# First stage of a two-layer decoder: raw input transposed, the norm's factors moved to the weights' split and to the evictions, half of the reordering on ScalarE

## The chip, the cores and the metric

One core of one Trainium2 chip runs the whole kernel in one launch. The metric is the device time of an execution in microseconds; the time before is the median of three runs. Durations are those of one profiled execution.

## What is computed

Two decoder layers over x (512 tokens, 1024 features, fp32). The change concerns the beginning of layer 0: the norm of x, and the projection to q, k and v with `w_qkv` for 12 heads in three groups of four.

```
def rms_norm(x, g):
    y = x32 * rsqrt(mean(x32 * x32, axis=-1) + EPS)
    return y * g
...
qkv = rms_norm(h, g[0]) @ w_qkv          # 1024 -> 3 * 768
q, k = rope(q), rope(k)                   # first 16 of 64 features of a head
# three groups of heads, (window, dilation) = (128,1), (512,4), (2048,16):
# banded softmax attention within each residue class of the dilation
o = concat(o_g * softmax over groups of the log denominators) @ w_o
h = h + rms_norm(o, g[1])
h = h + rms_norm(conv_ffn(rms_norm(h, g[2])), g[3])
# then a shared K/V and forget gates, forgetting attention, a second conv_ffn
```

## The kernel before

Every engine works through its own queue in order, and the order of the program's lines is the order of each queue (`manual_schedule`); waits between engines are semaphores that the framework puts in. SyncE issues nearly all loads.

**Precision.** A product of fp32 operands is made of three products in a rounded format (`mm3`, L263 to L266): each operand is split in a high part (a rounding copy on ScalarE) and a low part (operand less high part, on VectorE); the three are high·high, high·low and low·high.

**Weights.** `Weights` (L35 to L100) holds a list of pieces of 128x1024 fp32 (512 KB). `load` issues the transfers of a piece, `high` makes the high part on ScalarE (L57), `low` the low part on VectorE (L69), `split(n)` does both up to piece n, and `get` hands out the next pair after splitting `ahead` - 1 further ones. Pieces 0 to 3 are group 0's q and k columns (two chunks of 128 rows, kc, and 512 columns each), 4 and 5 group 0's v (four chunks of 256 columns each), 6 to 9 group 1's q and k, 10 to 13 group 2's, 14 to 17 the v of both.

**The start (L1252 to L1289).** x comes in four blocks of 128 tokens (`load_x`), in turn with the first pieces. The gain row is spread over 128 partitions by four products with a row of ones (L252); products of zeros before and after them (`warm_up`) keep TensorE busy. Per block b, `rstd_h` takes square, root and reciprocal, `normed` (L298) multiplies h by factor and gain on VectorE, `transpose_in` (L348) transposes the result on TensorE in two halves and splits each into xT's high part (ScalarE, L355) and low part (VectorE, L356). `qk0(b, pieces)` adds up block b's q and k of group 0 over the eight chunks. `qk_post` (L1071) copies them out on ScalarE and rotates on GpSimd.

**Groups 1 and 2** take the tokens by residue: `reorder` writes xT as xP, in which the tokens with the same remainder modulo 4 stand together. It is 16 copies of 128x512 that read every fourth element, all on GpSimd (L1060): blocks 0 and 1 after the second `qk_post`, blocks 2 and 3 after the last.

**What follows.** `v_proj0` makes group 0's v, and between its blocks the transposes of q and k (`qk_transpose`, copied out by VectorE at L1089). Then come the scores of blocks 0 and 1 (L1111; their softmax on VectorE L1096 and ScalarE L1097), group 1's q and k (`wide_proj(1)`), group 2's, and both v's. `down_sums` prepares sums of later weights all the while: SyncE loads, VectorE takes differences (L580 to L583), SyncE writes back. PSUM has eight banks for everything.

Of the kernel before, what the change touches and what calls it, by code (L numbers as in the profile page):

```python
# [9 lines left out]
F32 = mybir.dt.float32  # L10
# [5 lines left out]
D = 1024  # L16
T = 512
# [17 lines left out]
class Weights:  # L35
# [3 lines left out]
    def __init__(self, nc, new_raw, new_pair, pieces):  # L39
        self.nc, self.new_raw, self.new_pair, self.pieces = nc, new_raw, new_pair, pieces  # L40
        self.ahead, self.ahead_dma = 4, 2
        self.raw, self.ready, self.half_done = {}, {}, []
        self.n_dma = self.n_split = self.n_get = 0

# [8 lines left out]
    def high(self, minus=False):  # L53
        if self.n_split < len(self.pieces):
            self.load(self.n_split + 1 + self.ahead_dma)
            raw, pair = self.raw.pop(self.n_split), self.new_pair()
            self.nc.scalar.copy(pair[:, 0], raw)  # L57
            self.half_done.append((raw, pair))
            if minus:
                self.minus()  # L60
# [5 lines left out]
    def low(self):  # L66
        if self.half_done:
            raw, pair = self.half_done.pop()
            self.nc.vector.tensor_tensor(pair[:, 1], raw, pair[:, 0].bitcast(F32), ALU.subtract)  # L69
            self.ready[self.n_split] = (pair[:, 0], pair[:, 1])  # L70
            self.n_split += 1

# [31 lines left out]
def trunk_kernel(ctx, tc, x, norm_gains, w_qkv_a, w_o_a, w_q_b, w_o_b, kv_norm, w_kvf, b_f,  # L104
# [38 lines left out]
    for g in range(3):  # L143
        for s in range(4):
            def f(raw, g=g, s=s):
                v = raw.rearrange("p (k c) -> p k c", k=2)
                return [(v[:, :, 0:256], cols(wqkv, 2 * s, 2, g * 256, 256)),
                        (v[:, :, 256:512], cols(wqkv, 2 * s, 2, 768 + g * 256, 256))]
# [68 lines left out]

    eps_t = cst.tile([128, 1], F32, name="eps_t")
    dve.memset(eps_t, EPS)
    g_row = t4([1, D], name="g_row")  # L220
    sp.dma_start(g_row, norm_gains[0:1, 0, :])
    ones = sml.tile([1, 128], F32R, tag="ones", name="ones", bufs=1)
    dve.memset(ones.bitcast(F32), 1.0)

    zero = t2([128, 512], BF16, name="zero")
    dve.memset(zero, 0.0)
# [2 lines left out]
    def warm_up(n):  # L229
        for i in range(n):  # L230
            pe.matmul(warm, zero[:, 0:128], zero, start=True, stop=True)
# [10 lines left out]
    ident = cst.tile([128, 128], F32, name="ident")  # L242
    make_identity(nc, ident)

    gr = t4([1, D], F32R, name="gain_h"), t4([1, D], F32R, name="gain_l")
    dve.tensor_copy(gr[0], g_row)
    dve.tensor_tensor(gr[1], g_row, gr[0].bitcast(F32), ALU.subtract)
# [20 lines left out]
    def rstd_h(b, between=None):  # L268
        ss = small(1, "s1")
        junk = t2([128, D], BF16, name="junk")  # L270
        act.activation(junk, h[:, b, :], AF.Square, scale=1.0 / 32, accum_out=ss)
        sd = small(1, "sd")
        act.activation(sd, ss, AF.Sqrt, bias=eps_t)
        if between is not None:
            between()
        r = small(1, "rs")
        dve.reciprocal(r, sd)
        return r

    def rstd_shared(b):  # L280

        ss, s2 = small(1, "s1"), small(1, "vr")
        junk, junk2 = (t2([128, 512], BF16, name="junk") for _ in range(2))
        act.activation(junk, h[:, b, 0:512], AF.Square, scale=1.0 / 32, accum_out=ss)
        dve.scalar_tensor_tensor(junk2, h[:, b, 512:1024], 1.0 / 1024, h[:, b, 512:1024], ALU.mult, ALU.mult,
                                 accum_out=s2)
        dve.tensor_scalar(s2, s2, EPS, None, ALU.add)
        sd, r = small(1, "sd"), small(1, "rs")
        act.activation(sd, ss, AF.Sqrt, bias=s2)
        dve.reciprocal(r, sd)  # L290
        return r

# [752 lines left out]

    xT = new_xT("xa")
    xP = new_xT("xp")
    xn = {}

    def by_fourth(a, spec="p k (l r) -> p k r l"):  # L1050
        return a.rearrange(spec, r=4)

    def reorder(*blocks):
# [13 lines left out]
    def qk_post(g, b, o):  # L1067
        if b == 0:
            qks[g] = t8([128, 4, 8, HD], name=f"qk{g}")
        qk = qks[g][:, b]  # L1070
        act.copy(qk.rearrange("p a d -> p (a d)"), o)  # L1071
# [137 lines left out]
    def v_proj0(between):  # L1209
        banks = []  # L1210
        ws = [[t.rearrange("p (k c) -> p k c", k=4) for t in W.get()] for _ in range(2)]
        for b in range(4):
            if b % 2 == 0:
                banks.append(bank([128, 2, 256], name="v_ps"))
            for kc in range(KD):
                wh, wl = ws[kc // 4]
                ah, al = ax(0, b, kc)
                mm3(banks[b // 2][:, b % 2, :], ah, al, wh[:, kc % 4, :], wl[:, kc % 4, :],
                    kc == 0, kc == KD - 1)
            if b == 1:  # L1220
                V[0] = t4([128, 4, 256], name="V0")
            if b % 2:
                act.copy(V[0][:, b - 1:b + 1, :], banks[b // 2])
                for f in between[b // 2]:
                    f()

# [4 lines left out]
    W.ahead = 1  # L1231
    ws, qk_banks = {}, {}

    def norm0(b):
        xn[b] = normed(b, rstd_h(b), gain0)

    def transpose0(b, between=None):
        transpose_in(b, xn.pop(b), xT, between)

    def qk0(b, *pieces):  # L1240
        if b not in qk_banks:
            qk_banks[b] = bank([128, T], name="qk_ps")
        for s in pieces:
# [3 lines left out]
            for k in range(2):  # L1247
                kc = 2 * s + k
                ah, al = ax(0, b, kc)
                mm3(qk_banks[b], ah, al, wh[:, k, :], wl[:, k, :], kc == 0, kc == KD - 1)  # L1250

    xn[0] = normed(0, rstd_shared(0), gain0)  # L1252
    W.split(1)
    transpose0(0, L(W.split, 2))
    qk0(0, 0)
    W.high()
    r1 = rstd_h(1, W.low)
    qk0(0, 1)
    W.high()
    xn[1] = normed(1, r1, gain0)  # L1260
    W.low()
    qk0(0, 2)
    transpose0(1)
    qk0(0, 3)
    norm0(2)
    qk_post(0, 0, qk_banks[0])
    qk0(1, 0, 1, 2)
    transpose0(2)
    dve.tensor_reduce(same, ident.rearrange("p (a c) -> p c a", c=4), axis=mybir.AxisListType.X, op=ALU.add)
    dve.tensor_scalar(same, same, -NEG, NEG, ALU.mult, ALU.add)  # L1270
    dve.tensor_tensor(mask2.rearrange("p (a c) -> p a c", c=4),
                      mask0[:, 128:256].rearrange("p (a c) -> p a c", c=4),
                      same[:, None, :].to_broadcast([128, 32, 4]), ALU.add)
    norm0(3)
    qk0(1, 3)
    qk_post(0, 1, qk_banks[1])
    reorder(0, 1)
    qk0(2, 0, 1)
    transpose0(3)
    qk0(2, 2, 3)  # L1280
    W.split(5)
    qk_post(0, 2, qk_banks[2])
    qk0(3, 0, 1, 2, 3)
    W.ahead = 4
    W.split(6)
    qk_post(0, 3, qk_banks[3])
    sums = down_sums([(1, 6), (1, 7)], in_two, sp, 1, 3)
    next(sums)
    reorder(2, 3)  # L1289

    def wide_proj(g, name, post, between):

        banks = [bank([128, T], name=name) for _ in range(4)]
# [14 lines left out]
    def v_post(g, b, o):  # L1308
        if b == 0:
            for i in (1, 2):  # L1310
                V[i] = t4([128, 4, 256], name=f"V{i}")
        act.copy(V[1][:, b, :], o[:, 0:256])
        dve.tensor_copy(V[2][:, b, :], o[:, 256:512])
# [437 lines left out]
```

## Time and profile before

| | |
|---|---|
| time, median of 3 runs | 1112.1 us (1111.95 to 1112.55) |
| profiled execution | 1112.53 us |
| its span | 1110.8 us |
| TensorE busy | 1101.9 us (99%) |
| VectorE busy | 876.8 us (79%) |
| ScalarE busy | 660.6 us (59%) |
| GpSimd busy | 214.9 us (19%) |
| first product with a weight | 9.17 us |
| first product of group 0's v | 35.16 us |

A row of a timeline gives the start in us, the time in us, engine, line, operation, what is written from what, the shape and the count; in brackets stands how long the engine sat idle before it and what ended that. A row of the groups gives the busy time in us, the mean of one in ns, and the idle time before them. PE is TensorE, PEld its weight loads, DVE VectorE, ACT ScalarE, POOL GpSimd, SP SyncE.

### The profile page before, as it was taken

How to read it: one execution, taken by the hardware profiler on the slowest of the kernel's cores; microseconds unless marked ns; L12 is line 12 of the kernel's file. 1: busy time of each engine (PE TensorE's matmuls, PEld its weight loads, DVE VectorE, ACT ScalarE, POOL GpSimd, SP SyncE). 2: the span in 40 equal slices, each digit the busy share in tenths (PEclk: the TensorE clock that was granted, in tenths of full speed). 3: DMA queues.
4: the chain of work that ended last, by engine and by line, in shares of the span. 5: the costliest groups of instructions: out<-in, count | busy, mean ns of one | idle time of the engine just before them, and what ended most of it. 6: DMA issues, size and time to landing. Idle time of an engine off the chain costs nothing.

```text
span 1110.8 us, 18056 instructions
## 1 busy us (share of the span) xinstructions
PE 1101.9 (99%) x6610; PEld 952.9 (86%) x6610; DVE 876.8 (79%) x1484; ACT 660.6 (59%) x1088; POOL 214.9 (19%) x313
## 2 busy tenths in 40 slices
PE   9999999999999999999999999999999999999997
PEld 6988889899999988888878788789999999988886
DVE  6587788888788689997686676868887787779894
ACT  5444565656666747576451587756556666747572
POOL 2832001311111211000000455500411111211000
PEclk9999999999999999999999999999999999999999
DMA  9599864468878979894448434593379888989872
GB/s 325 173 340 410 325 181 135 86 180 191 210 190 185 249 254 321 292 324 112 133 152 281 163 107 119 169 286 114 83 180 212 192 186 193 229 265 322 315 246 76
DMA packets 184242, 236.26 MB, mean 213 GB/s; under 512 B 11673, under 2 KB 131465, under 8 KB 184154
## 3 DMA queue, kind: packets, MB, share of 16 engines
q1 hardware_dynamic: 169210, 182.94, 50.6%
q0 software_dynamic: 14944, 52.18, 20.6%
q8 instruction: 52, 0.85, 0.3%
q14 instruction: 36, 0.29, 0.1%
HBM read 166.08 MB, written 39.63 MB: 185 GB/s over the span
## 4 chain that ended last, share of the span: by engine, by line
PE 94%; DVE 2%; DMA 1%; issue 1%; ACT 1%; POOL 1%; DVEq 0%; SPq 0%; POOLq 0%; ACTq 0%
PE up L266 12%; PE up L265 12%; PE up L264 12%; PE acc L264 8%; PE acc L265 8%; PE acc L266 8%; PE v_ps L264 2%; PE v_ps L266 2%; PE v_ps L265 2%; PE qk_ps L265 2%; PE qk_ps L264 2%; PE qk_ps L266 2%; PE q_ps L264 1%; PE first L266 1%; PE first L264 1%; PE first L265 1%
## 5 line engine op out<-in xcount | busy, mean ns | idle before, releaser
L264 PE MATMUL acc<-w 128*128 128x512 f32 (+1 forms) x311 | 120.6, 388 | 0.3 <-DVE mix L326 0.3
L266 PE MATMUL acc<-w 128*128 128x512 f32 (+1 forms) x311 | 120.4, 387 | 0.0
L69 DVE TENSOR_TENSOR w<-wraw,w 128x1024 fp32r<-128x1024 f32 x74 | 97.5, 1334 | 27.1 <-ACT w L57 26.7
L57 ACT CAST w<-wraw 128x1024 fp32r<-128x1024 f32 x94 | 96.9, 1050 | 22.7 <-PE v_ps L265 6.9
L265 PE MATMUL acc<-w 128*128 128x512 f32 (+1 forms) x267 | 103.2, 387 | 0.0
L266 PE MATMUL up<-xsh,w 128*128 128x256 f32 x352 | 99.7, 283 | 0.1
L264 PE MATMUL up<-xsh,w 128*128 128x256 f32 x352 | 99.6, 283 | 0.0
L265 PE MATMUL up<-xsl,w 128*128 128x256 f32 x352 | 99.6, 283 | 0.0
L614 ACT ACTIVATE bb<-up,conv 128x512 f32<-128x512 f32 x80 | 59.7, 776 | 59.0 <-DVE up L1001 48.2
L265 PE MATMUL up<-xbl,w 128*128 128x512 f32 (+1 forms) x276 | 93.5, 339 | 0.0
L265 PE MATMUL up<-xcl,w 128*128 128x512 f32 (+1 forms) x276 | 93.5, 339 | 0.0
L264 PE MATMUL up<-xbh,w 128*128 128x512 f32 (+1 forms) x276 | 93.5, 339 | 0.0
L266 PE MATMUL up<-xbh,w 128*128 128x512 f32 (+1 forms) x276 | 93.5, 339 | 0.0
L264 PE MATMUL up<-xch,w 128*128 128x512 f32 (+1 forms) x276 | 93.5, 339 | 0.0
L266 PE MATMUL up<-xch,w 128*128 128x512 f32 (+1 forms) x276 | 93.4, 338 | 0.0
L264 PEld LDWEIGHTS acc<-w 128*128 128x128 f32 x311 | 58.4, 188 | 12.6 <-DVE mix L326 0.7
L266 PEld LDWEIGHTS acc<-w 128*128 128x128 f32 x311 | 58.4, 188 | 11.9
L266 PEld LDWEIGHTS up<-xsh,w 128*128 128x128 f32 x352 | 67.6, 192 | 0.3 <-DMA w<-wsum 0.3
L265 PEld LDWEIGHTS up<-xsl,w 128*128 128x128 f32 x352 | 67.6, 192 | 0.0
L264 PEld LDWEIGHTS up<-xsh,w 128*128 128x128 f32 x352 | 67.6, 192 | 0.0
L615 DVE SCALAR_TENSOR_TENSOR bb<-up,conv,bb 128x511 f32<-128x511 f32 x80 | 59.5, 744 | 6.2 <-ACT bb L614 6.0
L617 DVE SCALAR_TENSOR_TENSOR bb<-up,conv,bb 128x510 f32<-128x510 f32 x80 | 59.9, 749 | 2.8
(313 smaller groups left out, 3118.7 us busy)
## 6 DMA issues: line engine op xcount, KB each, us to landing
wraw<-in_w_up_dram SPq DMA_DIRECT2D x88, 512.0 KB, 5.6
w<-wraw POOLq DMA_DIRECT2D x32, 512.0 KB, 6.4
dT<-dsums SPq DMA_DIRECT2D x28, 512.0 KB, 7.6
w<-wsum POOLq DMA_DIRECT2D x24, 512.0 KB, 5.8
dsums<-in_w_down_dram SPq DMA_DIRECT2D x22, 512.0 KB, 7.6
dsums<-in_w_down_dram SPq DMA_DIRECT2D x44, 256.0 KB, 5.5
hD<-hc POOLq DMA_DIRECT2D x44, 256.0 KB, 6.9
dact<-hD SPq DMA_DIRECT2D x44, 256.0 KB, 5.6
```

Source lines behind the costliest of these rows:

```text
L57: self.nc.scalar.copy(pair[:, 0], raw)
L69: self.nc.vector.tensor_tensor(pair[:, 1], raw, pair[:, 0].bitcast(F32), ALU.subtract)
L264: pe.matmul(o, ah, bh, start=first, stop=False, skip_group_check=shared)
L265: pe.matmul(o, ah, bl, start=False, stop=False, skip_group_check=shared)
L266: pe.matmul(o, al, bh, start=False, stop=last, skip_group_check=shared)
L614: act.activation(bb[:, s, :], ps, AF.Identity, bias=cp[:, 3, ch:ch + 1], scale=cp[:, 2, ch:ch + 1])
L615: dve.scalar_tensor_tensor(bb[:, s, 1:], ps[:, :T - 1], cp[:, 1, ch:ch + 1], bb[:, s, 1:], ALU.mult, ALU.add)
L617: dve.scalar_tensor_tensor(bb[:, s, 2:], ps[:, :T - 2], cp[:, 0, ch:ch + 1], bb[:, s, 2:], ALU.mult, ALU.add)
```

## The change

x is transposed as it lands. The gain, which belongs to a feature, goes into the split of the weights of group 0, 1 and 2 (pieces 0 to 17): a piece is split chunk by chunk, the high part by an activation with the chunk's gains as scale, the low part by a scalar-tensor-tensor. The gains come as eight columns through one small transpose. The reciprocal root, which belongs to a token, goes into the evictions of q, k and v as a scale; for groups 1 and 2 it takes a round trip through DRAM (`factors_out`) to come in the order of xP. The pieces of q and k are loaded as two transfers by chunk instead of by q and k. TensorE's order of the first products is by chunks over blocks 0 and 1; pieces 4 and 5 are split before the third block; blocks 2 and 3 are reordered by ScalarE.

```
@@ Weights.high / Weights.low
-            self.nc.scalar.copy(pair[:, 0], raw)
+            scales = self.scales.get(self.n_split)
+            if scales is None:
+                self.nc.scalar.copy(pair[:, 0], raw)
+            else:
+                for i, g in enumerate(scales):
+                    s = slice(i * 1024 // len(scales), (i + 1) * 1024 // len(scales))
+                    self.nc.scalar.activation(pair[:, 0, s], raw[:, s], AF.Identity, scale=g)
...
+                    self.nc.vector.scalar_tensor_tensor(pair[:, 1, s], raw[:, s], g, pair[:, 0, s].bitcast(F32),
+                                                        ALU.mult, ALU.subtract)
@@ loads and gains
     load_x(0)
+    W.load(2)
+    load_x(1)
     W.load(3)
-    load_x(1)
+    load_x(2)
     W.load(4)
-    load_x(2)
...
-    gain0 = [bank([128, 512], name="gain00") for _ in range(2)]
-    warm_up(4)
-    for part in range(2):
-        for i in range(2):
-            pe.matmul(gain0[i], ones, gr[part][:, i * 512:(i + 1) * 512], start=part == 0, stop=part == 1)
-    warm_up(4)
+    warm_up(3)
+    pg0 = bank([128, 8], name="g_ps")
+    pe.transpose(pg0, g_row, ident[:8, :8])
+    gcol0 = sml.tile([128, 8], F32, tag="gcol0", name="gcol0", bufs=1)
+    dve.tensor_copy(gcol0, pg0)
+    warm_up(5)
...
+    for s in range(4):
+        for n in (s, 6 + s, 10 + s, 14 + s):
+            W.scales[n] = columns(2 * s, 2 * s + 1)
+    for s in range(2):
+        W.scales[4 + s] = columns(*range(4 * s, 4 * s + 4))
@@ factors, reordering, evictions
+    def rstd0(b):
+        ss, sd = small(1, "s1"), small(1, "sd")
+        junk = t2([128, D], BF16, name="junk")
+        act.activation(junk, h[:, b, :], AF.Square, scale=1.0 / 32, accum_out=ss)
+        act.activation(sd, ss, AF.Sqrt, bias=eps_t)
+        dve.reciprocal(rt[:, 0, b:b + 1], sd)
+    def factors_out():
+        sp.dma_start(rd.rearrange("(b p) -> p b", p=128), rt[:, 0])
+        sp.dma_start(rt[:, 1], rd.rearrange("(l r) -> l r", r=4))
...
-                    pool.tensor_copy(dst, src.bitcast(F32))
+                    copy(dst, src.bitcast(F32))
...
-        act.copy(qk.rearrange("p a d -> p (a d)"), o)
+        act.activation(qk.rearrange("p a d -> p (a d)"), o, AF.Identity, scale=factor(g, b))
@@ the start
+    pts = transposed0(0)
+    warm_up(2)
+    high0(0, pts, 0)
+    low0(0, pts, 0)
     W.high()
+    W.low()
+    high0(0, pts, 1)
+    qk0(0, 0, 1)
     W.high()
     W.low()
+    low0(0, pts, 1)
     qk0(0, 2)
+    pts = transposed0(1)
+    for i in range(2):
+        high0(1, pts, i)
+        low0(1, pts, i)
     qk0(0, 3)
+    rstd0(0)
+    W.split(3)
+    qk0(1, 0, 1, 2, 3)
+    split0(2)
+    rstd0(1)
+    qk0(0, 4, 5)
+    W.split(4)
+    qk0(1, 4, 5)
+    split0(3)
+    qk0(0, 6, 7)
     qk_post(0, 0, qk_banks[0])
+    W.split(5)
...
+    qk0(1, 6, 7)
     qk_post(0, 1, qk_banks[1])
+    W.split(6)
+    rstd0(2)
+    rstd0(3)
+    factors_out()
+    reorder(pool.tensor_copy, 0, 1)
+    qk0(2, *range(8))
     qk_post(0, 2, qk_banks[2])
+    qk0(3, *range(8))
     W.ahead = 4
     qk_post(0, 3, qk_banks[3])
+    reorder(act.copy, 2, 3)
     sums = down_sums([(1, 6), (1, 7)], in_two, sp, 1, 3)
     next(sums)
```

(In `qk0` of the change the numbers are chunks of 128 rows, two to a piece; `transposed0` is the eight transposes of a block, `high0` and `low0` are the two parts of one half, `split0(b)` is all of these.)

More of the change, by code (lines that the diff above doesn't have):

```diff
@@ L41, in __init__ @@
         self.ahead, self.ahead_dma = 4, 2
+        self.scales = {}
         self.raw, self.ready, self.half_done = {}, {}, []
@@ L145, in f @@
             def f(raw, g=g, s=s):
-                v = raw.rearrange("p (k c) -> p k c", k=2)
-                return [(v[:, :, 0:256], cols(wqkv, 2 * s, 2, g * 256, 256)),
-                        (v[:, :, 256:512], cols(wqkv, 2 * s, 2, 768 + g * 256, 256))]
+                v = raw.rearrange("p (k t c) -> p k t c", k=2, t=2)
+                src = wqkv.rearrange("(k p) (t c) -> p k t c", p=128, c=256)
+                return [(v[:, k], src[:, 2 * s + k, g:g + 4:3, :]) for k in range(2)]
             add(f)
@@ L243, in trunk_kernel, with columns @@
     make_identity(nc, ident)
[L245 to L253 removed]
+    warm_up(3)
[4 more added lines that the diff above has]
+    warm_up(5)
+    def columns(*ks):
+        return [gcol0[:, k:k + 1] for k in ks]
+    for s in range(4):
[3 more added lines that the diff above has]
+        W.scales[4 + s] = columns(*range(4 * s, 4 * s + 4))
     mask0 = cst.tile([128, 256], F32, name="mask0")
@@ L276, in rstd_h @@
         r = small(1, "rs")
[L277 to L289, printed above, removed]
         dve.reciprocal(r, sd)
@@ L1047, in trunk_kernel, with factor, reorder @@
     xP = new_xT("xp")
-    xn = {}
+    rt = sml.tile([128, 2, 4], F32, tag="rt", name="rt", bufs=1)
+    rd = tc.dram_tile([T], F32, name="rd")
+    def rstd0(b):
[7 more added lines that the diff above has]
+        sp.dma_start(rt[:, 1], rd.rearrange("(l r) -> l r", r=4))
+    def factor(g, b):
+        return rt[:, min(g, 1), b:b + 1]
     def by_fourth(a, spec="p k (l r) -> p k r l"):
         return a.rearrange(spec, r=4)
-    def reorder(*blocks):
+    def reorder(copy, *blocks):
         for i in range(2):
@@ L1222, in v_proj0 @@
             if b % 2:
-                act.copy(V[0][:, b - 1:b + 1, :], banks[b // 2])
+                for i in range(2):
+                    act.activation(V[0][:, b - 1 + i, :], banks[b // 2][:, i], AF.Identity, scale=factor(0, b - 1 + i))
                 for f in between[b // 2]:
@@ L1232, in trunk_kernel, with transposed0, high0, low0 @@
     ws, qk_banks = {}, {}
[L1234 to L1240, printed above, removed]
+    def transposed0(b):
+        pts = []
+        for i in range(2):
+            pt = bank([128, 4, 128], name="xt_ps")
+            for k in range(4):
+                pe.transpose(pt[:, k, :], h[:, b, (4 * i + k) * 128:(4 * i + k + 1) * 128], ident)
+            pts.append(pt)
+        return pts
+    def high0(b, pts, i):
+        act.copy(xT[0][i][:, :, b * 128:b * 128 + 128], pts[i])
+    def low0(b, pts, i):
+        s = slice(b * 128, b * 128 + 128)
+        dve.tensor_tensor(xT[1][i][:, :, s], pts[i], xT[0][i][:, :, s].bitcast(F32), ALU.subtract)
+    def qk0(b, *kcs):
         if b not in qk_banks:
             qk_banks[b] = bank([128, T], name="qk_ps")
-        for s in pieces:
+        for kc in kcs:
+            s, k = kc // 2, kc % 2
             if s not in ws:
@@ L1246, in qk0, with split0 @@
             wh, wl = ws[s]
[L1247 to L1255, printed above, removed]
+            ah, al = ax(0, b, kc)
+            mm3(qk_banks[b], ah, al, wh[:, k, :], wl[:, k, :], kc == 0, kc == KD - 1)
+    def split0(b):
+        pts = transposed0(b)
+        for i in range(2):
+            high0(b, pts, i)
+            low0(b, pts, i)
+    pts = transposed0(0)
+    warm_up(2)
+    high0(0, pts, 0)
+    low0(0, pts, 0)
     W.high()
-    r1 = rstd_h(1, W.low)
-    qk0(0, 1)
+    W.low()
+    high0(0, pts, 1)
+    qk0(0, 0, 1)
     W.high()
-    xn[1] = normed(1, r1, gain0)
     W.low()
+    low0(0, pts, 1)
     qk0(0, 2)
-    transpose0(1)
+    pts = transposed0(1)
+    for i in range(2):
+        high0(1, pts, i)
+        low0(1, pts, i)
     qk0(0, 3)
-    norm0(2)
+    rstd0(0)
[8 more added lines that the diff above has]
+    qk0(0, 6, 7)
     qk_post(0, 0, qk_banks[0])
-    qk0(1, 0, 1, 2)
-    transpose0(2)
+    W.split(5)
     dve.tensor_reduce(same, ident.rearrange("p (a c) -> p c a", c=4), axis=mybir.AxisListType.X, op=ALU.add)
@@ L1311, in v_post @@
                 V[i] = t4([128, 4, 256], name=f"V{i}")
-        act.copy(V[1][:, b, :], o[:, 0:256])
-        dve.tensor_copy(V[2][:, b, :], o[:, 256:512])
+        act.activation(V[1][:, b, :], o[:, 0:256], AF.Identity, scale=factor(1, b))
+        dve.tensor_scalar(V[2][:, b, :], o[:, 256:512], factor(2, b), None, ALU.mult)
     down0 = down_sums([*[(0, j) for j in range(ND)], (1, 8)], in_one, sp, 1, 1)
```

23 lines of the change are left out of this document (8 added, 15 removed).

## The prediction, made before the change ran

> **What bounds the kernel now.** I read the page first (span, busy shares, chain), then the timelines of TensorE, ScalarE and VectorE over the first 70 us, then the groups by line and form for the price of each kind of instruction. The page:
>
> ```profile
> span 1110.8 us, 18056 instructions
> ...
> PE 1101.9 (99%) x6610; PEld 952.9 (86%) x6610; DVE 876.8 (79%) x1484; ACT 660.6 (59%) x1088; POOL 214.9 (19%) x313
> ...
> PE 94%; DVE 2%; DMA 1%; issue 1%; ACT 1%; POOL 1%; DVEq 0%; SPq 0%; POOLq 0%; ACTq 0%
> ```
>
> TensorE is busy for 99% of the span and is 94% of the chain. The change takes away no product with a weight; so it can win only where TensorE now stands still or repeats warm-ups, and lose only where it is made to wait. The waits are in the first 16 us (weight loads of TensorE, last column what ended the idle time):
>
> ```profile
> 9.17 0.19 PEld L264 LDWEIGHTS qk_ps<-w,xah 128*128 128x128 f32 x1 [0.30 <-ACT xah L355]
> 9.90 0.19 PEld L266 LDWEIGHTS qk_ps<-w,xal 128*128 128x128 f32 x1 [0.43 <-DVE xal L356]
> 11.38 0.19 PEld L265 LDWEIGHTS qk_ps<-w,xah 128*128 128x128 f32 x1 [0.49 <-DVE w L69]
> 13.11 0.19 PEld L265 LDWEIGHTS qk_ps<-w,xah 128*128 128x128 f32 x1 [0.51 <-DVE w L69]
> 15.76 0.19 PEld L265 LDWEIGHTS qk_ps<-w,xah 128*128 128x128 f32 x1 [0.43 <-DVE w L69]
> ```
>
> The first product starts at 9.17; four more waits follow, all on VectorE. After 15.76 nothing is idle up to the end of the first group's q/k products, which I call E: the first value product, at 35.16. The change is judged by when E falls, and by what happens between E and about 65 us.
>
> ```profile
> 1.35 1.89 PE L231 MATMUL warm<-zero 128*128 128x512 bf16 x4 [1.35 <-DVE zero L226]
> 7.41 1.70 PE L348 MATMUL xt_ps<-ident,xn 128*128 128x128 f32 x8 [0.16 <-DVE xn L298]
> 10.23 0.39 PE L264 MATMUL qk_ps<-w,xah 128*128 128x512 f32 x1
> 10.46 0.39 PE L265 MATMUL qk_ps<-w,xah 128*128 128x512 f32 x1
> 26.11 1.03 PE L348 MATMUL xt_ps<-ident,xn 128*128 128x128 f32 x8
> 26.90 0.48 PE L264 MATMUL qk_ps<-w,xah 128*128 128x512 f32 x1
> 35.16 0.28 PE L264 MATMUL v_ps<-w,xah 128*128 128x256 f32 x1
> 48.50 1.68 PE L1111 MATMUL s_ps<-qkT 64*128 64x128 f32 x16
> 63.80 1.32 PE L1133 MATMUL pT_ps<-ident,p 128*128 128x128 f32 x8
> ```
>
> Prices of TensorE: from 26.90 to 35.16 lie 36 products (half of block 2, all of block 3), so 8.26/36 = 0.23 us each; eight transposes take 26.90 - 26.11 = 0.8 us (the first eight took 1.70, twice that).
>
> **The change, part 1: the start.** Block 0 no longer waits for its norm: raw x is transposed as it lands. Prices of the other engines:
>
> ```profile
> 4.90 0.63 ACT L284 ACTIVATE junk<-h 128x512 bf16<-128x512 f32 x1 [2.67 <-DMA h<-in_x_dram]
> 6.72 1.05 ACT L57 CAST w<-wearly 128x1024 fp32r<-128x1024 f32 x1 [0.53 <-DMA wearly<-in_w_qkv_a_dram]
> 8.53 0.59 ACT L355 CAST xah<-xt_ps 128x512 fp32r<-128x512 f32 x1 [0.77 <-PE xt_ps L348]
> 11.39 1.07 ACT L271 ACTIVATE junk<-h 128x1024 bf16<-128x1024 f32 x1
> 12.35 0.20 ACT L271 ACTIVATION_READ_ACCUMULATOR junk<-h 128x1 f32 x1
> 12.58 0.29 ACT L273 ACTIVATE sd<-s,eps_t 128x1 f32<-128x1 f32 x1
> ```
> ```profile
> 9.15 0.69 DVE L356 TENSOR_TENSOR xal<-xt_ps,xah 128x512 fp32r<-128x512 f32 x1
> ```
> ```profile
> L614 ACT ACTIVATE bb<-up,conv 128x512 f32<-128x512 f32 x80 | 59.7, 776 | 59.0 <-DVE up L1001 48.2 <-PE up L266 10.8
> L506 ACT ACTIVATE xqh<-nT,gcol 128x512 fp32r<-128x512 f32 x8 | 5.4, 720 | 0.0
> ```
> ```profile
> L507 DVE SCALAR_TENSOR_TENSOR xql<-nT,gcol,xqh 128x512 fp32r<-128x512 f32 x8 | 5.6, 746 | 0.0
> ```
>
> L506 and L507 are just the new split of a half piece: 0.72 on ScalarE, 5.6/8 = 0.70 a step on VectorE. Block 0 of x is there at 4.90. Ahead of its transposes stand eight warm-ups (two times 1.89 at most from 1.35) and the small transpose of the gains: they start at 5.1. In 7.41 to 8.53 the first half took 1.1 to reach ScalarE, so its high part runs 6.2 to 6.8, its low part 6.8 to 7.5. Piece 0 has landed by 6.72; its two scaled halves end on ScalarE at 7.4 and 8.0, on VectorE at 8.2 and 8.9. ScalarE then does the second high part of x (8.5) and piece 1 (9.2, 9.8); VectorE ends piece 1 at 9.9 and 10.6, the second low part at 11.3. TensorE, after two more warm-ups, starts its first product at 7.65, waits for lows at 8.2 and 9.9, and has nine products by 10.5. From there it follows its own queue: transposes of block 1 to 11.3, three products to 12.0, block 1's first twelve (low part of x at 12.6, a wait of 0.1) to 14.9, transposes of block 2 (15.7), twelve (18.5), transposes of block 3 (19.3), twelve (22.1), and 48 of blocks 2 and 3: E at 33.2. ScalarE's other work on the way (block 0's square and root, 1.07 + 0.29 and a read of 0.2, then piece 2) ends at 15.0, VectorE's low of piece 2 at 15.1 and 15.8, for products at 15.7 and 16.4; piece 3 likewise ends at 19.4 and 20.1 for 19.3 and 20.0. So VectorE is just in time, with no room; I keep 0.8 both ways on E.
>
> Transfers: between 4.90 and 6.72 one piece of 512 KB landed, 1.8 us; by that slow pace x1, third behind x0 instead of fourth, lands at 10.4 for 10.5, x2 (fifth) at 14.0 for 14.9; no wait. **Term 1: E goes from 35.16 to 33.2, -2.0 us.** The removed gain products (L252) and warm-ups lie ahead of x's landing and are worth nothing by themselves.
>
> **Part 2: the reordering on ScalarE.** Blocks 2 and 3 become eight copies of 128x512 with every fourth element read, in ScalarE's queue behind the last q/k eviction. Behind them now stand the splits of pieces 6 to 8, and on VectorE, behind their lows, the copies of the transposed q/k that the first scores wait for.
>
> ```profile
> 35.36 0.59 ACT L1071 COPY qk<-qk_ps 128x512 f32<-128x512 f32 x1 [3.90 <-PE qk_ps L266]
> 35.84 2.95 ACT L57 CAST w<-wraw 128x1024 fp32r<-128x1024 f32 x3
> ```
> ```profile
> 36.93 3.91 DVE L69 TENSOR_TENSOR w<-wraw,w 128x1024 fp32r<-128x1024 f32 x3 [4.22 <-ACT w L57]
> 48.17 1.29 DVE L1089 COPY qkT<-qkT_ps 128x512 f32<-128x512 f32 x2 [5.33 <-PE qkT_ps L1086]
> 57.16 1.22 DVE L69 TENSOR_TENSOR w<-wraw,w 128x1024 fp32r<-128x1024 f32 x1
> 62.88 0.42 DVE L1096 CUSTOM_DVE_ANT_0 p<-s_ps,mask 128x256 f32<-128x256 f32 x1 [0.58 <-PE s_ps L1111]
> ```
> ```profile
> 50.00:60.00 10.00, 10.00 (x47) 8.20 (x46) 9.73 (x24) 5.98 (x22) 1.22 (x2) 1.00 0.82 294
> ```
>
> Now: the lows end at 40.8, and VectorE idles 5.33 before the next q/k copies at 48.17, which is E + 13.0. From there to 62.88 it is full (9.73 of 10 us in the window, third busy column), and at 62.88 only 0.58 early for the second scores, whose banks TensorE needs back: the eight transposes right behind them, at 63.80, took 1.32 instead of 0.8. So a delay of VectorE past E + 13.0 passes to TensorE almost whole; the 0.58 is used up by pieces 9 and 10, whose lows cost 1.4 instead of 1.22 each.
>
> With p the step of one copy: eviction starts at E + 0.2, takes about 0.7 (776 ns of L614 less an overlap of 0.1 that three casts of 1.05 in 2.95 show), copies 8p, first half split 0.72, six lows of 0.70 = 4.2, two q/k copies 1.25: E + 7.1 + 8p. That is E + 13.0 at p = 0.74. No row shows ScalarE reading every fourth element. Bounds: a plain copy, 0.59 less 0.1 = 0.49; and the nearest on ScalarE, L1190, which writes every fourth element:
>
> ```profile
> L1190 ACT COPY ow<-o_ps 128x512 f32<-128x512 f32 x4 | 4.1, 1134 | 0.3 <-PE o_ps L1185 0.3
> ```
> ```profile
> L1269 DVE TENSOR_REDUCE same<-ident 128x4 f32<-128x128 f32 x1 | 0.4, 369 | 0.0
> L1271 DVE TENSOR_TENSOR mask<-mask,same 128x128 f32<-128x128 f32 x1 | 0.3, 291 | 0.1
> ```
>
> L1190 gives p = 1.03. The only read at that stride with a price is VectorE's L1269: 128 elements in 369 ns against 291 for a plain 128 (L1271), 0.6 ns an element more; for 512 that adds 0.31 to 0.59, p = 0.80 to 0.82. I take 0.82, between the ends, since it is a read. **Term 2: 8 x 0.82 + 7.1 - 13.0 = +0.6 us** (0 to +2.3). [...]
>
> **Part 3: the rest.** Evictions with a factor cost about 0.2 more on ScalarE (776 against 0.59), behind a block's products that take 1.4 (six of 0.23); twelve later pieces cost 0.3 more on ScalarE and 0.26 on VectorE: hidden by pieces split up to four ahead. Pieces 4 and 5, in quarters, end about 26, before E. SyncE's queue stops for the factors' round trip: the last root is ready at about 28.7 (ScalarE ends piece 5 at 25.6, then two squares, reads and roots of 1.55); the first small transfer takes at most the 5.6 of the row below, I take it, and the load of piece 8 behind it as much again, so that it lands by 42 for its split at about E + 10:
>
> ```profile
> wraw<-in_w_up_dram SPq DMA_DIRECT2D x88, 512.0 KB, 5.6
> ```
>
> Nothing, with 1 us of cover; if that is gone, it delays VectorE's lows one for one. GpSimd loses eight copies; it released nobody at the time (below zero: nothing to gain).
>
> **Sum.** The profiled execution took 1112.53 (span 1110.8), 0.4 above the median of 1112.1. 1112.5 - 2.0 + 0.6 = 1111.1, so 1110.7 against the median.
>
> **Rivals.** *Cheap copies.* If ScalarE reads at that stride at full pace, p = 0.49 and term 2 is nothing: 1110.1; with E another 0.8 earlier, 1109.3. For it: the one slow row writes, and the destination here is runs of 32.
>
> *Dear copies.* L1190's price: 1112.1 - 2.0 + 2.3 = 1112.4, no difference; then VectorE decides, from p = 0.74 on.
>
> *TensorE stays at its half pace, slower than before.* The first transposes went at 0.21 each, the products from 10.23 at 0.23, full pace: the pace changed between. The page's granted clock does not show it. If in the changed start the change of pace comes not before 12.7, ten products (0.2 more each), eight transposes (0.8 more) fall in the slow stretch: E 2.6 later, 1113.3; with dear copies 1115. It decides if the pace has not changed by the ninth product. For it: the row of warm-ups is split by a transpose of 8 rows, and products wait twice. Against: by my walk it stands still for less than 0.5 us between 5.1 and 10.5, and before, with as many waits, the pace changed all the same. [...]
>
> *It doesn't do what it says*: the factors only move from x to weights and evictions, and if each of VectorE's ten steps up to 11.3 comes 0.2 later, E stays at 35.2: 1112.7.
>
> **How the numbers follow.** A measurement of this kernel can tell about 0.2% (2.2 us) from no change. Forecast (p about 0.8, E 32.4 to 34.0): 0.45, of it 0.12 faster by more than that. Cheap copies: 0.27, of it 0.22 faster, with E early. Dear copies or no gain at E: 0.13, of it 0.05 slower. Half pace: 0.15, all slower if it meets any further wait. Together 0.34 faster, 0.46 same, 0.20 slower. Range: from cheap copies with an early E and the earlier pace (1108.6) to half pace with the forecast's copies (1113.6 with 0.3 for E).
>
> **What would show it.** First product near 7.65 with lows of pieces 0 and 1 as the waits; E near 33.2; ScalarE's copies of 0.9 us between E + 0.9 and E + 7.5; the first scores at E + 14. Wrong if the copies take 0.6 or 1.1, if transposes after 9.3 still take 1.7 for eight, or if E moves by less than 1.

## The result and the profile after

The changed kernel took 1117.4 us, median of six runs (1116.96 to 1118.28); the kernel before, run beside it, 1112.2 (1111.76 to 1112.73, six runs). The ratio is 1.0045, 95% interval 1.0035 to 1.0056: slower by about 5 us, where 1110.7 was forecast and 1113.6 was the upper end. The profiled execution took 1117.56. From the page of the profile after, its span and the busy times:

```profile
span 1115.8 us, 18088 instructions
PE 1102.2 (99%) x6609; PEld 954.5 (86%) x6609; DVE 875.5 (78%) x1493; ACT 677.4 (61%) x1120; POOL 203.4 (18%) x305
```

The span is 5.0 longer, and TensorE is busy for as long as before, within 0.3. So 4.7 of the 5.0 is standing still, which one finds on its timeline; work done at a slower pace counts as busy, and some of that shows below as well. Rows of the kernel after (start, time, engine, line, operation; idle time and its end in brackets), from its start and from the first scores:

```profile
7.44 0.50 PE L283 MATMUL qk_ps<-w,xah 128*128 128x512 f32 x1 [0.37 <-ACT w L64]
8.23 0.50 PE L284 MATMUL qk_ps<-w,xah 128*128 128x512 f32 x1 [0.28 <-DVE w L82]
9.94 0.50 PE L284 MATMUL qk_ps<-w,xah 128*128 128x512 f32 x1
10.51 1.03 PE L1261 MATMUL xt_ps<-ident,h 128*128 128x128 f32 x8
14.90 1.04 PE L1261 MATMUL xt_ps<-ident,h 128*128 128x128 f32 x8
...
33.03 0.28 PE L283 MATMUL v_ps<-w,xah 128*128 128x256 f32 x1
45.41 1.03 PE L1107 MATMUL qkT_ps<-ident,qk 128*128 128x128 f32 x8
51.22 3.09 PE L1132 MATMUL s_ps<-qkT 64*128 64x128 f32 x16 [4.77 <-DVE qkT L1110]
67.26 2.10 PE L1132 MATMUL s_ps<-qkT 64*128 64x256 f32 x16
```

Up to 33.03 the change did what it was to do: E, the first value product, came 2.13 earlier than at 35.16. Then TensorE finished the transposes of q and k at 46.4 and stood still for 4.77 us until VectorE had copied them; 16 products of the first scores, 1.68 before, took 3.09. The second scores began at 67.26; before, they began at 61.71:

```profile
61.71 2.10 PE L1111 MATMUL s_ps<-qkT 64*128 64x256 f32 x16
```

Counted from E the loss is plain. First scores: E + 18.19 after, E + 13.34 before, so 4.85 later. From there to the second scores: 16.04 against 13.21, so 2.83 more. Together 7.68; with E 2.13 earlier that is the 5.55 between 67.26 and 61.71. The span is longer by 5.0 only, since 1048.5 lie behind the second scores against 1049.1; this remainder goes from 1048.4 to 1050.0 over the twelve profiles of this document, so the 0.55 means nothing by itself.

What stood before the wait, followed back on the chain of waits of the kernel after:

```profile
29.72 9.43 DMA rd<-rt
39.16 0.34 SPq L1066
...
40.97 0.43 SPq L50
41.45 7.58 DMA wraw<-in_w_qkv_a_dram
49.06 0.73 ACT w L64
49.81 0.75 DVE w L82
50.56 0.61 DVE qkT L1110
51.22 3.09 PE s_ps L1132 x16
```

The first line is the transfer of the factors to DRAM: 2 KB, issued at 29.72, landed 9.43 us later. SyncE, which must not issue the read before, stood at L1066 all that time; behind it in its queue were the loads of `down_sums` and the six transfers of pieces 8 to 10. The second half of piece 8 landed at 49.03; its split, VectorE's low part and VectorE's copy of q and k follow one behind the other, each released by the one before. The timeline of ScalarE shows the same point from its side:

```profile
41.09 1.18 ACT L1081 CAST xpl<-xal 128x512 fp32r<-128x512 f32 x1
42.14 2.59 ACT L64 ACTIVATE w<-wraw,gcol 128x512 fp32r<-128x512 f32 x4
48.29 1.48 ACT L64 ACTIVATE w<-wraw,gcol 128x512 fp32r<-128x512 f32 x2 [3.56 <-DMA wraw<-in_w_qkv_a_dram]
```

Its last copy of the reordering ends at 42.3, pieces 6 and 7 are split at once, and for piece 8 it waits 3.56 for the load. The windows (busy time of PE, PEld, DVE, ACT and POOL, the granted clock, the DMA share, GB/s), first of ten us and then of four, show the two other sides of it:

```profile
30.00:40.00 10.00, 10.00 (x74) 9.46 (x73) 0.00 (x0) 7.18 (x8) 7.59 (x13) 1.00 0.05 1
40.00:50.00 10.00, 6.44 (x55) 6.20 (x53) 3.68 (x6) 6.40 (x10) 0.00 (x0) 1.00 0.79 273
50.00:60.00 10.00, 8.78 (x35) 7.04 (x36) 9.34 (x28) 7.38 (x23) 0.00 (x0) 0.66 1.05 390
```
```profile
34.00:38.00 4.00, 4.00 (x36) 4.00 (x35) 0.00 (x0) 4.00 (x5) 3.59 (x9) 1.00 0.00 0
38.00:42.00 4.00, 4.00 (x36) 4.00 (x36) 0.00 (x0) 4.00 (x5) 0.00 (x0) 1.00 0.00 0
```

From 30 to 40 the DMA engines move 1 GB/s: up to 39.16 none of the kernel's transfers is in flight but the small write. From 34 to 42 they move nothing at all, though the write counts as landed only at 39.15; what it waits for in those five us the trace doesn't show. From 50 to 60 the granted clock is 0.66, and in windows of one us it is 0.50 from 51 to 57: after its wait TensorE ran at half pace, which is the 2.83.

### The profile page after: what moved, and what is told of

It is laid out like the page before. It is cut to its first block, busy times and chain, and to the rows that moved or that the text cites. A ratio compares the mean times of both kernels' runs of the same rounds, so it can differ in the third digit from the quotient of the medians.

```text
span 1115.8 us, 18088 instructions
## 1 busy us (share of the span) xinstructions
PE 1102.2 (99%) x6609; PEld 954.5 (86%) x6609; DVE 875.5 (78%) x1493; ACT 677.4 (61%) x1120; POOL 203.4 (18%) x305
## 4 chain that ended last, share of the span: by engine, by line
PE 92%; DMA 2%; DVE 1%; POOL 1%; issue 1%; ACT 1%; SPq 0%; DVEq 0%; POOLq 0%; ACTq 0%
PE up L283 13%; PE up L284 13%; PE up L285 12%; PE acc L283 8%; PE acc L284 8%; PE acc L285 8%; PE v_ps L283 2%; PE v_ps L285 2%; PE v_ps L284 2%; PE q_ps L283 1%; PE qk_ps L283 1%; PE first L285 1%; PE first L283 1%; PE first L284 1%; PE qk_ps L285 1%; PE qk_ps L284 1%
## 5 line engine op out<-in xcount | busy, mean ns | idle before, releaser
L78 DVE TENSOR_TENSOR w<-wraw,w 128x1024 fp32r<-128x1024 f32 x62 | 82.2, 1341 | 22.7 <-ACT w L60 22.3
L60 ACT CAST w<-wraw 128x1024 fp32r<-128x1024 f32 x82 | 84.5, 1049 | 18.6 <-PE v_ps L284 6.9
```

## The experiments

The theory from the traces: the small write holds the loads up, the copies on ScalarE are dear (a step of 1.04), and the length of the wait brings the half pace. Its rivals: VectorE is late because of the copies alone; or SyncE's standing still is the cost and not the write as such. Since E wanders by 0.6 between kernels, the table gives the positions behind E. The wait is TensorE's idle time before the first scores.

| kernel | E | first scores | wait | they take | second scores | ratio to before, 95% |
|---|---|---|---|---|---|---|
| before | 35.16 | E + 13.34 | none | 1.68 | E + 26.55 | |
| after | 33.03 | E + 18.19 | 4.77 | 3.09 | E + 34.23 | 1.0045 (1.0035 to 1.0056) |
| read_late | 32.70 | E + 16.47 | 3.06 | 2.77 | E + 31.40 | 1.0024 (1.0014 to 1.0033) |
| pool_only | 32.98 | E + 17.76 | 4.35 | 3.09 | E + 32.47 | 1.0032 (1.0019 to 1.0045) |
| late_pool | 33.03 | E + 16.77 | 3.36 | 2.18 | E + 31.70 | 1.0022 (1.0012 to 1.0031) |
| clock_kept | 33.11 | E + 17.47 | filled | 1.74 | E + 30.78 | 1.0017 (1.0008 to 1.0026) |
| gather_read | 32.88 | E + 14.61 | 1.20 | 1.83 | E + 27.99 | 0.9990 (0.9981 to 0.9999) |
| gather_pool | 33.03 | E + 16.73 | 3.32 | 1.83 | E + 30.09 | 1.0023 (1.0014 to 1.0032) |
| loads_first | 33.10 | E + 14.61 | 1.20 | 1.83 | E + 28.00 | 0.9996 (0.9987 to 1.0006) |
| loads_gather_pool | 33.34 | E + 13.34 | none | 1.68 | E + 26.55 | 0.9976 (0.9967 to 0.9985) |
| pool_busy | 33.19 | E + 18.89 | 5.48 | 3.09 | E + 34.56 | 1.0053 (1.0039 to 1.0067) |
| loads_gather_act | 32.76 | E + 14.61 | 1.20 | 1.83 | E + 28.01 | 0.9996 (0.9987 to 1.0006) |

**read_late: SyncE doesn't stop.** The read of the factors is issued between the products of the second stage, behind the loads; the write and ScalarE's copies stay.

```diff
     def factors_out():
         sp.dma_start(rd.rearrange("(b p) -> p b", p=128), rt[:, 0])
+
+    def factors_in():
         sp.dma_start(rt[:, 1], rd.rearrange("(l r) -> l r", r=4))
...
-        [L(p_transpose, 0, 0)],
+        [L(p_transpose, 0, 0), factors_in],
```

> Theory A (SyncE's queue): the factors' write takes 9.4 us to land and the read behind it keeps SyncE from issuing the load of piece 8, which lands at 48.3 and holds, through ScalarE's split and VectorE's low, the copies of q/k for the first scores. With the read issued after those loads, piece 8 lands before 40, ScalarE no longer waits for a transfer, and only the dear copies (1.05 us a step) are left: first scores at E + 14.9 instead of E + 18.2, TensorE waits about 1.4 us instead of 4.8 and keeps its pace; total 1111.8 to 1113. Theory B (ScalarE's copies alone set the wait, the transfer is hidden behind them): scores stay at E + 17 or later, total 1116 to 1117.4.

1115.38 us, which neither theory had; the ratio fell by 0.0021 only, to 1.0024. SyncE's timeline, then windows of four us:

```profile
29.39 0.37 SPq L1065 DMA_DIRECT2D rd<-rt  x1
29.80 0.51 SPq L581 DMA_DIRECT2D dsums<-in_w_down_dram  x1
...
34.55 9.28 SPq L50 DMA_DIRECT2D wraw<-in_w_qkv_a_dram  x6
```
```profile
30.00:34.00 4.00, 4.00 (x24) 3.53 (x23) 0.00 (x0) 1.18 (x3) 4.00 (x5) 1.00 0.59 19
34.00:38.00 4.00, 4.00 (x36) 4.00 (x35) 0.00 (x0) 4.00 (x5) 3.25 (x9) 1.00 0.51 35
38.00:42.00 4.00, 4.00 (x37) 4.00 (x36) 0.00 (x0) 4.00 (x5) 0.00 (x0) 1.00 0.46 36
42.00:46.00 4.00, 4.00 (x35) 3.87 (x34) 2.74 (x4) 2.84 (x5) 0.00 (x0) 1.00 1.02 371
```

The loads now leave right behind the write, but they crawl: 19 to 36 GB/s until 42, where the same loads later make 371, and issuing six of them takes SyncE 9.28. So SyncE's stop is only a part of it (2.83 at the second scores): the loads behind this write get little through until 42, 12.6 us after it was issued. How that comes about the trace doesn't show.

**gather_read: the same write in longer runs.** The four factors of a partition go to DRAM side by side (16 bytes instead of four times 4 bytes), and four reads bring them into the order of xP. SyncE waits as in the change.

```diff
-        sp.dma_start(rd.rearrange("(b p) -> p b", p=128), rt[:, 0])
-        sp.dma_start(rt[:, 1], rd.rearrange("(l r) -> l r", r=4))
+        sp.dma_start(rd.rearrange("(p b) -> p b", b=4), rt[:, 0])
+        for b in range(4):
+            sp.dma_start(rt[b * 32:b * 32 + 32, 1, :], rd.rearrange("(l r b) -> b l r", r=4, b=4)[b])
```

> The factors are written as runs of 16 bytes and brought into order on the read, by four small transfers. Theory A2 (the write's 512 pieces of 4 bytes fill the queues for some 10 us, so that the loads behind them crawl even where SyncE doesn't wait for them): the write lands in under 4 us, piece 8 before 42, ScalarE waits for no transfer; the dear copies are left, first scores at E + 14.9, TensorE waits about 1.4 us; total 0.3 us under to 0.6 over before. Theory A1 (any write and wait at this place costs it, whatever its pieces): the scores stay at E + 16.5 or later, total 2.5 over before or more.

1111.57, ratio 0.9990: this edit alone took 0.0055 off, 6.1 us, and left the kernel 1 us faster than before. Its DMA issues (KB each, us to landing) and SyncE's timeline:

```profile
rd<-rt SPq DMA_DIRECT2D x1, 2.0 KB, 1.4
```
```profile
29.57 0.34 SPq L1065 DMA_DIRECT2D rd<-rt  x1
31.00 3.63 SPq L1067 DMA_DIRECT2D rt<-rd  x4
...
36.27 3.34 SPq L50 DMA_DIRECT2D wraw<-in_w_qkv_a_dram  x6
```

The same 2 KB land in 1.4 us instead of 9.43. Pieces 8 to 10 leave at 36.27, ScalarE doesn't wait for a load any more, and TensorE's wait is 1.20, with no half pace behind it (granted clock 1.00 from 50 to 60, where the change has 0.66). By the diff the write of the change has 512 pieces of 4 bytes, that of gather_read 128 of 16. The profile agrees: it counts 528 packets under 512 bytes from 29.5 to 40 in the change and 144 from 29.5 to 31.2 here, in both the pieces and 16 more. Four times as many pieces took 6.7 times as long. But the number alone can't be the reason: the four reads of gather_read take the factors back in 512 pieces of 4 bytes (576 such packets from 31.2 to 36), and the loads behind them move at 331 GB/s from 38 to 42. What was slow is 4-byte pieces written to DRAM; whether by their size, their number or both, no run separates.

**loads_first: the loads ahead of the write.** Everything as in the change, but pieces up to 10 and the first loads of `down_sums` are issued before the factors.

```diff
     rstd0(3)
+    W.load(11)
+    sums = down_sums([(1, 6), (1, 7)], in_two, sp, 1, 3)
+    next(sums)
     factors_out()
...
     reorder(act.copy, 2, 3)
-    sums = down_sums([(1, 6), (1, 7)], in_two, sp, 1, 3)
-    next(sums)
```

> The change with the loads of pieces 8 to 10 and of the first sums issued ahead of the factors' round trip, the write in pieces of 4 bytes as it was, ScalarE's copies as they were. If the load of piece 8 is all that the round trip hurts, the scores come at E + 14.9 and the total is 0.3 under to 0.6 over before; if the clogged queues also hurt the next loads (the second sums, pieces 11 and on), VectorE's sums come late and the total is 1 to 3 over.

E + 14.61 and E + 28.00, like gather_read to 0.01 though the write is nearly as slow as in the change (the read leaves 8.55 us behind it). So the write does no harm by itself, nor do late factors; it harms the loads that it stands ahead of. The ratios of the two, 0.9996 and 0.9990, can't be told apart.

**clock_kept: only the half pace.** Nineteen products of zeros, added work, fill TensorE's gap before the first scores; all else as in the change.

```diff
+    def keep_warm(n=19):
+        zz = t2([128, 512], BF16, name="zz")
+        pool.memset(zz, 0.0)
+        o = bank([128, 512], name="warm2")
+        for i in range(n):
+            pe.matmul(o, zz[:, 0:128], zz, start=True, stop=True)
...
-             [L(qk_transpose, 0, 2), L(qk_transpose, 0, 3), L(scores, 0, 0), L(scores, 0, 1), L(next, sums), L(next, down0)]])
+             [L(qk_transpose, 0, 2), L(qk_transpose, 0, 3), keep_warm, L(scores, 0, 0), L(scores, 0, 1), L(next, sums), L(next, down0)]])
```

> The change as it is, with 19 products of zeros on TensorE in the gap before the first scores (work added, nothing else changed). If the slow pace after the gap (scores 3.09 us instead of 1.68, seven products at 0.43) is lost time of its own, the scores take 1.7 again and the total falls by about 2.8 us, to 1114.3 to 1115. If the wait alone counts and VectorE is next anyway, the total stays within 0.6 of 1117.4.

```profile
46.57 4.05 PE L1257 MATMUL warm<-zz 128*128 128x512 bf16 x18
50.58 1.74 PE L1132 MATMUL s_ps<-qkT 64*128 64x128 f32 x16
```

(The trace has 18 of the 19.) On TensorE's timeline the scores still begin late, at E + 17.47, 0.72 less than in the change because the load of piece 8 landed earlier by about as much; but they take 1.74, and from them to the second scores it is 13.31 instead of 16.04. The granted clock from 50 to 60 is 1.00 instead of 0.66. The slow pace after the wait was worth 2.7 us, and it came of standing still. The ratio fell by 0.0028.

**pool_only and late_pool: the reordering back on GpSimd.** The first undoes ScalarE's half of the reordering and nothing else; the second does that on top of read_late.

```diff
-    reorder(act.copy, 2, 3)
+    reorder(pool.tensor_copy, 2, 3)
```

> All of the reordering on GpSimd, the factors' round trip as in the change. Theory A: ScalarE splits pieces 6 and 7 eight us earlier and then waits longer for piece 8, which still lands at about 48; first scores at 51 as in the change, total 1116.8 to 1117.6. Theory B: the wait goes, total 1110 to 1111.

> Read issued late and all of the reordering on GpSimd. Theory A: both limits gone, TensorE waits nowhere after 13 us, E's gain of 2.1 us arrives whole: 1109.8 to 1110.6; GpSimd ends its copies near 46, before group 1's first product at 48. Theory B: the same as with the reordering alone moved back. If neither is all of it, the total stays above 1111.5 and another wait shows between E and 70 us.

pool_only: 1116.70, 0.1 under theory A's range, first scores 0.43 earlier behind E than in the change and a ratio of 1.0032; the load still ends the wait. late_pool, 1115.27, is not better than read_late, against theory A. Its groups of waits say why (us in total, times, longest):

```profile
ACT w L64 <- DMA wraw<-in_w_qkv_a_dram: 10.4, 2, 9.1
```

A ScalarE freed of eight copies only waits longer, 10.4 us in all, for loads that crawl (35 and 34 GB/s in the two windows from 34 to 42). While the write stands in the way, the place of the copies can't be priced.

**gather_pool: both undone.** gather_read with the same edit as pool_only.

> The same write and read, and all of the reordering on GpSimd. Theory A2: no wait of TensorE after 13 us; E's gain of 2.1 us arrives whole, total 1.8 to 2.4 under before. Theory A1: like the late read with the reordering on GpSimd, 2.7 over before.

This surprised me: 1.0023, slower than gather_read by 0.0033. TensorE waited 3.32 instead of 1.20. On its chain of waits:

```profile
41.87 0.73 ACT w L64
...
42.63 0.25 DVE w L82
42.88 5.49 issue
48.37 0.74 DVE w L82
49.11 0.61 DVE qkT L1111
```

ScalarE is early: it splits piece 8 at 41.87, when in gather_read it has just done its last copy and begins with piece 6 (41.99). But VectorE's two low parts took 6.48 instead of some 1.4. "issue" here is time in which VectorE waited for nothing that the profile shows. On the timelines GpSimd was copying without a pause from 39.33 to 47.90. Two groups of VectorE from 33 to 50 us (busy, mean ns; the first row is gather_read, the second gather_pool):

```profile
L82 DVE SCALAR_TENSOR_TENSOR w<-wraw,gcol,w 128x512 fp32r<-128x512 f32 x6 | 4.1, 744 | 13.2 <-ACT w L64 13.2
```
```profile
L82 DVE SCALAR_TENSOR_TENSOR w<-wraw,gcol,w 128x512 fp32r<-128x512 f32 x6 | 9.9, 1700 | 9.5 <-ACT w L64 9.5
```

The profile is of the shortest of this kernel's ten executions, 1113.61 with a median of 1115.07, so the positions show less than the ratio: 2.1 behind E. Over a whole execution the mean granted clock was 0.999 in the two shortest, 0.997 or 0.998 in the next seven and 0.995 in the longest (1117.85). That looks as if others lost pace behind the wait as well, which the profiled one did not; without their traces it is not shown.

**pool_busy: GpSimd's copies by themselves.** gather_read, in which ScalarE does the reordering, with nine more copies on GpSimd into a tile that nobody reads.

```diff
+    for n in range(9):
+        spare = t2([128, 4, 4, 32], name="spare")
+        pool.tensor_copy(spare, by_fourth(xT[0][n % 2][:, :, 256:384]).bitcast(F32))
     reorder(act.copy, 2, 3)
```

> The kernel gather_read with nine more copies of 128x512 on GpSimd, of every fourth element, into a spare tile that nobody reads, right behind the start of the second stage. [...] Theory (in gather_pool VectorE's low parts of pieces 6 to 8 were slow because GpSimd was copying at the same time): those low parts, 4.06 us in gather_read, take 7 us or more, the first scores start 3 us or more behind 47.49, and the time is 1.5 to 3.5 us over gather_read, 0.0 to +0.25% beside the kernel before. Rival (gather_pool was slow because the real copies on GpSimd came late, or by chance): low parts of 4.0 to 4.4 us, scores at 47.5 to 48, the time as gather_read, ratio 0.999.

Timelines of GpSimd and VectorE:

```profile
37.86 9.70 POOL L1339 COPY spare<-xah 128x512 f32<-128x512 f32 x9
43.09 5.02 DVE L82 SCALAR_TENSOR_TENSOR w<-wraw,gcol,w 128x512 fp32r<-128x512 f32 x1 [13.24 <-ACT w L64]
48.69 1.40 DVE L82 SCALAR_TENSOR_TENSOR w<-wraw,gcol,w 128x512 fp32r<-128x512 f32 x2
52.08 3.09 PE L1133 MATMUL s_ps<-qkT 64*128 64x128 f32 x16 [5.48 <-DVE qkT L1111]
```

VectorE's first low part started at 43.09 and took 5.02: it ended at 48.11, 0.55 after the last of GpSimd's copies (47.56), and the five behind it, with no copy beside them, took 3.31 together. The six took 8.33 instead of 4.06, as the theory had it, and no result waited for GpSimd. The time was under-priced: 0.0063 over gather_read, 7 us, not 1.5 to 3.5, since the wait of 5.48 brought the half pace with it (3.09 for the scores). GpSimd's copies kept their 1.08 each (9.70 by 9). VectorE's copies of q and k were not held: in loads_gather_pool, below, two of them took 1.29 at 46.35, in the middle of GpSimd's copies, as in the kernel before (1.29 at 48.17). The low part reads the raw weights and their high part, the copy one bank of PSUM; whether that is the difference that counts no run shows.

**loads_gather_pool and loads_gather_act: the change without its two costs.** The first has the loads ahead, the longer runs of gather_read in `factors_out` and all reordering on GpSimd; the second is the same without the last edit, so that ScalarE reorders blocks 2 and 3. Only that lies between the two.

```diff
+    W.load(11)
+    sums = down_sums([(1, 6), (1, 7)], in_two, sp, 1, 3)
+    next(sums)
     factors_out()
...
-    reorder(act.copy, 2, 3)
+    reorder(pool.tensor_copy, 2, 3)
```

> Loads ahead, runs of 16 bytes, all of the reordering on GpSimd: every suspect removed. TensorE waits nowhere after 13 us; 1.8 to 2.6 under before. If it is not below gather_pool, the load of piece 8 had room already.

> The kernel loads_gather_pool with blocks 2 and 3 reordered by ScalarE, as the change does it: the one edit between the two is that half of the reordering, with the round trip of the factors out of the way in both. Theory (one copy by ScalarE at this stride costs a step of 1.05 us and pushes the splits of pieces 6 to 8, VectorE's low parts and its q/k copies back): the first scores start at E + 14.4 to 14.8 instead of E + 13.3, TensorE waits 1.0 to 1.4 us for the q/k copies, and the time is 0.7 to 1.6 us over loads_gather_pool, ratio 0.9983 to 0.9992 beside the kernel before. Rival (the copies on ScalarE cost nothing once the transfer is short, because it took GpSimd's interference out in exchange): scores within 0.3 us of E + 13.3 and the ratio of loads_gather_pool, 0.9976, within 0.0004.

loads_gather_pool took 1110.03, 0.9976 of before: faster than the kernel before by 2.7 us (1.7 to 3.7). On VectorE's, TensorE's and GpSimd's timelines:

```profile
34.88 5.01 DVE L82 SCALAR_TENSOR_TENSOR w<-wraw,gcol,w 128x512 fp32r<-128x512 f32 x6 [4.88 <-ACT w L64]
40.55 1.11 POOL L1082 CAST xph<-xah 128x512 fp32r<-128x512 f32 x1
46.68 1.68 PE L1133 MATMUL s_ps<-qkT 64*128 64x128 f32 x16
```

With pieces 6 to 8 there early and ScalarE free, VectorE's low parts are done at 39.9, before GpSimd's second round of copies starts at 40.55, and both positions behind E are those of before to 0.01. Here the early E is kept whole.

loads_gather_act has E + 14.61 and E + 28.01: the copies on ScalarE cost 1.27 at the first scores and 1.46 at the second. The span is 1.7 longer (1110.0 against 1108.3): the 1.46, less 0.58 by which E happens to come earlier, and 0.8 behind the second scores, which is within what that remainder varies. The ratio, 0.9996, lies 0.0020 higher, a little more than was expected; by the intervals it could be 0.0002 to 0.0039.

## Why the prediction was wrong, by its own steps

- **Term 1 was right.** -2.0 was forecast, -2.13 measured. First product at 7.44 for 7.65, the products that need low parts at 8.23 and 9.94 for 8.2 and 9.9, block 1's transposes at 10.51 for 10.5, block 2's at 14.90 for 14.9, E at 33.03 for 33.2. That the total fits to 0.13 is partly luck, since E differs by 0.6 between kernels with this start. Those transposes took 1.03 for eight, so the rival of a TensorE that stays at half pace in the start did not come. The range's lower end counts 0.7 for an earlier change of pace, and that rival starts from a 12.7; no run shows either. In the kernel after, block 0's eight transposes still took 1.61 (1.70 before), two products of zeros at 6.48 only 0.59 (five took 2.31 at 2.82), and E lay 0.17 before the forecast's 33.2.
- **Part 3 failed, and decided.** It priced SyncE's stop at nothing with 1 us of cover, by "at most the 5.6" of a 512 KB load for the first small transfer, and had piece 8 landed by 42. The write took 9.43; piece 8's split began at 48.29. The step that failed is the bound: a big load's time was taken as an upper end for a transfer of 2 KB that is written in 512 pieces of 4 bytes. By its terms piece 8 lands at 28.7 + 5.6 + 5.6 = 39.9, rounded up to 42; it landed at 49.03, 9.1 later: 3.8 by the write, 2.0 by the load (7.58), 2.3 for issuing the read and the loads ahead, 1.0 by the last root. The row it used has 512 KB in runs of 512 bytes; the diff shows 512 elements that lie apart. And it stopped at the landing: the next mechanism, a wait of TensorE long enough for the half pace, was weighed at the start only. Undone alone, in gather_read, the transfer is worth 6.24 at the second scores (34.23 less 27.99): 3.58 of wait and 2.66 of pace.
- **Term 2 had the right mechanism and the wrong size.** It took a step of 0.82 between copies and +0.6; the step is 1.04 (eight copies from 33.82 to 42.14), and the cost 1.27 to 1.46. These are the dear copies, L1190's price, where writes at that stride were the nearest row on the same engine; VectorE's row was the wrong one to interpolate from. At L1190's price, 1.03, the formula makes the term +2.3, and it was 1.27 to 1.46. The formula itself held: E + 7.1 + 8 x 1.04 gives E + 15.4 for the second pair of q/k copies, and in gather_read it is E + 15.1 (46.76, two copies later). What failed is "passes to TensorE almost whole": 2.1 late there, 1.20 waited, since the first scores need only the first of the copies.
- **GpSimd "released nobody at the time"** was the wrong question. Taking eight copies off it also took away what holds VectorE's low parts (six take 9.9 in gather_pool, 4.1 in gather_read); nothing in the step looked at that. Put back without moving the low parts (gather_pool), it cost 2.1 at the second scores more than ScalarE's copies do. The kernel before shows the contest the other way round: two of GpSimd's copies, started beside VectorE's low parts of pieces 4 and 5, took 2.1 instead of 1.1.

```profile
28.81 1.78 DVE L69 TENSOR_TENSOR w<-wearly,w 128x1024 fp32r<-128x1024 f32 x1 [0.15 <-ACT w L57]
31.49 1.23 DVE L69 TENSOR_TENSOR w<-wearly,w 128x1024 fp32r<-128x1024 f32 x1 [0.90 <-ACT w L57]
```
```profile
29.45 2.12 POOL L1060 CAST xpl<-xal 128x512 fp32r<-128x512 f32 x1
31.51 2.16 POOL L1060 CAST xph<-xah 128x512 fp32r<-128x512 f32 x1
```

- **Sum.** Forecast -2.0 + 0.6 + 0; measured at the second scores -2.13 + 1.44 (gather_read's 27.99 less 26.55) + 6.24 = +5.55, and 0.55 less behind them, within what that remainder varies: +5.0, the difference of the spans.
- **Two slips in the working changed nothing.** The half pace's own terms, ten products at 0.2 and 0.8 for the transposes, make 2.8 and not 2.6. And the 1.32 of the eight transposes at 63.80 stands against 1.03 for eight in the same kind of row (26.11), not against 0.8, which is from start to start.

## What to carry to other kernels

Here the same 2 KB took 9.43 us to DRAM as 512 pieces of 4 bytes and 1.4 as 128 of 16. So price a small write by the size and number of its separate pieces and not by its bytes, and ask what stands behind it in its queue; if loads do, issue them first or lay the pieces side by side (the two brought the first scores from E + 18.19 to E + 14.61 each). In five of the six profiles here in which TensorE waited 3.06 to 5.48 us, the wait cost 1.5 to 2.8 more in pace, so price the wait and what follows it together. Before work is moved between GpSimd and another engine, look at which VectorE instructions run beside it: here GpSimd's copies held the low parts (8.33 and 9.9 for six instead of 4.1), and not the copies of q and k (1.29 for two).

## What the runs showed that was not expected

- 512 pieces of 4 bytes took 9.43 us to DRAM (8.55 to 9.44 until the read in the four kernels whose SyncE waited for it), 128 pieces of 16 bytes 1.4; loads issued behind the first moved at 19 to 36 GB/s until 42.
- One VectorE instruction of 0.74 was held for 5.02 by a train of GpSimd copies, across the borders between them.
- The half pace doesn't follow from the length of the wait alone: with 1.20 the scores took 1.83, with 3.06 2.77, with 3.32 1.83, with 3.36 2.18, with 4.35 and more 3.09. In windows of one us the clock is 0.50 for 3.4 us in read_late, late_pool and pool_only and for 6.8 in the change and pool_busy (means from 50 to 60: 0.83 or 0.84, and 0.66); in gather_pool's profile, with a wait of 3.32, it stays at 1.00 (the products from 51.86 to 56.87 come every 0.23). Between the first and the second scores that cost 1.72, 1.72 and 1.50, and 2.83 and 2.46. So how long the scores take doesn't tell the whole price: in late_pool the clock fell only after 51, when they were nearly done. What sets the length of these stretches no run shows.
